# A two-layer decoder trunk in float32 on one core: gathers of the heavy experts five blocks ahead, and two 8 KB tiles as a fifth pair of split weights

## Chip, cores and metric

The kernel runs on one core of one Trainium2 chip. The metric is device time in microseconds (us) of one execution; the median of three executions of the kernel before is 1350.78 us (1350.66 to 1352.81).

## The reference, cut to what matters

256 tokens of width 1024 pass through two residual layers in float32: attention beside a short convolution with a dense SwiGLU, then a gated recurrence with a mixture of experts. The change touches the mixture alone, the last and longest stage:

```python
logits = xf @ w_router                       # 256 tokens, 8 experts
top_logits, top_idx = lax.top_k(logits, 2)
gates = softmax(top_logits)
...
xb = xf[tok]                                 # the tokens of one expert
hb = silu(xb @ w_gate[e]) * (xb @ w_up[e])   # 1024 -> 3584
yb = hb @ w_down[e]                          # 3584 -> 1024
out = zeros.at[row_tok].add(yb * row_gate)
```

Each expert has three matrices of 1024 x 3584 floats. All eight are read whatever the routing: 336 loads of 1 MB.

## The kernel before, in words

**Products in two parts.** A float32 weight tile of 128 x 2048 is split into a high part H, which ScalarE (ACT) writes rounded (L258), and a low part L, the rest, which VectorE (DVE) subtracts (L259). TensorE (PE) multiplies with both. `prepare(n)` (L995) fetches load `n` and splits it.

**Memory of a load.** A load lands in a ring place. There are five tiles of the pool `ring` (`N_RING`, L31) and, by `source` (L978 to 993), two 8 KB tiles of the pool `t8` (`b8`) used in turn with them: seven places in all. Once, in the first round of nine, two loads land in 4 KB halves. A place is free again when DVE has made L from it. The parts H and L go to one of four pairs (`N_HL`, L32; `pair`, L221); a pair is free again when PE has used it.

**Blocks.** The experts are ranked on the chip by their number of tokens. Three heavy ones (0, 3, 6, up to 128 tokens) are worked with 3 matmuls per product, five light ones (1, 2, 4, 5, 7, up to 64) with 2. One block is 512 of the 3584 columns of one expert: 12 pieces (four each of gate `g`, up `u`, down `d`) and 6 loads. The order of the 56 blocks is written out in `experts` (L920 to 928): three heavy blocks, then light, heavy, light again and again. The down pieces of a block come after the gate and up pieces of the next. Expert 1 ends with block 12 and expert 0 with block 13, expert 2 with block 23, experts 3 and 4 with blocks 34 and 33, expert 5 with block 44.

**Other work, by pieces.** The main loop (L1233) multiplies piece `n`, copies out what is pending (`flush`), does what `at` has put down for this piece, and then prepares further loads, up to `(n + 1) // 2 + AHEAD`. All this is one fixed order for each engine. The other work is:

- `choose` (L1011) makes on DVE the matrix of zeros and ones that picks an expert's tokens, and takes the tiles for them;
- `gather` (L1029), four calls, multiplies the tokens with it (L1040 for heavy, L1052 for light experts) into a PSUM tile `pz`, which ACT copies out (L1042, L1057);
- `factors` and `back` (L1062, L1072) prepare the gates and the way back;
- `turn` and `turn_light` (L1111, L1119), five pieces after a block's last `u`, transpose the hidden values through `pz`;
- `out_parts` (L1141) splits an expert's finished sum on ACT and DVE, and `combine` (L1150), four calls from five pieces later on, multiplies it back to the tokens through `pz` (L1155, L1156), and DVE adds it to the residual (L1158).

There are two `pz` tiles. Whoever wants one waits until the one before the last has been read by ACT or DVE.

`experts` places the gathers of a unit of experts that starts at block `s` with `n = s - 3`: `choose` at the last `u` piece of block `n`, the four gathers at pieces `u0`, `u2`, `d0`, `d2` of block `n + 1` (that is `pn(n + 1, "u", 2 * b)`).

The last weights land at about 1326 us; then come the last products, two experts' ends and the output.

Of the kernel before, what the change touches and what calls it, by code (L numbers as in the profile page):

```python
# [9 lines left out]
F32 = mybir.dt.float32  # L10
# [20 lines left out]
N_RING = 5  # L31
N_HL = 4  # L32
# [18 lines left out]

AHEAD = N_HL
FIRST = 1
SECOND = 2
TURN = 5
BACK = 5

TURNS8 = N_RING + 2  # L60
TURNS4 = TURNS8 + 2
ROUNDS = 1

CUT = 4

# [50 lines left out]
def body(ctx, tc, x_d, w_d, prm_d, bv_d, rt_d, out_d):  # L116
# [14 lines left out]
    def nm(s):  # L131
        uid[0] += 1
        return f"{s}_{uid[0]}"

    def b8(dt=F32R):
        return t8.tile([P, 2048], dt, tag="b8", name=nm("b8"))

    def b4(dt=F32):
        return t4.tile([P, 1024], dt, tag="b4", name=nm("b4"))
# [60 lines left out]
    def load(k, w=None, cuts=1):  # L200
        o, n = OFF[k]
        if w is None:
            w = ring.tile([P, 2048], F32, tag="w", name=nm("w"))
        src = w_d[o:o + n * P].rearrange("(p n) -> p n", p=P)
        m = n // cuts
        for c in range(0, n, m):
            nc.sync.dma_start(w[:, c:c + m], src[:, c:c + m])
        return w

    def halves(k):  # L210

        o, n = OFF[k]
        src = w_d[o:o + n * P].rearrange("(p n) -> p n", p=P)
        ws = b4(), b4()
        for i in range(2):
            nc.sync.dma_start(ws[i], src[:, i * 1024:(i + 1) * 1024])
        return ws

    ps = [P0]

    def pair():  # L221
        return [hl.tile([P, 2048], F32R, tag=t, name=nm(t)) for t in "HL"]
# [3 lines left out]
    def split(w, j, n=1024):  # L226

        if j == 0:
            pairs[w.name] = pair()
        c = slice(j * n, (j + 1) * n)  # L230
        h, l = (a[:, c] for a in pairs[w.name])
        with tc.high_priority(offset=ps[0]):
            A.activation(h, w[:, c], AF.Copy)  # L233
            V.tensor_sub(l, w[:, c], h.bitcast(F32))  # L234
        return h, l
# [20 lines left out]
    def hl_of(src, oh, ol):  # L256

        A.activation(oh, src, AF.Copy)  # L258
        V.tensor_sub(ol, src, oh.bitcast(F32))  # L259
# [12 lines left out]
    def norm_factor(spread=True):  # L272

        tot = b2()
        for i in range(4):
            xi = x_sb[:, 2 * i:2 * i + 2, :].rearrange("p k s -> p (k s)")
            if i == 0:
                A.activation(tot, xi, AF.Square)
            else:
                sq = b2()  # L280
                A.activation(sq, xi, AF.Square)
                V.tensor_add(tot, tot, sq)
        p = pz()
        for t in range(2):
            for j in range(2):
                T.matmul(p[:, t:t + 1], tot[:, j * S + t * P:j * S + (t + 1) * P], ones[:, 0:1],
                         start=j == 0, stop=j == 1)
        r = cst.tile([P, 2], F32, name=nm("r"))
        y = rsqrt(p[:, 0:2], 2, 1.0 / D)
        V.tensor_copy(r, y)  # L290
        if not spread:
            return r, None
        dg = b1(F32)
        p = pz()
        for t in range(2):
            V.tensor_scalar(dg[:, t * P:(t + 1) * P], ident, y[:, t:t + 1], None, OP.mult)
            T.matmul(p[:, t * P:(t + 1) * P], ones, dg[:, t * P:(t + 1) * P], start=True, stop=True)
        rs = b1(F32)
        A.activation(rs, p[:, 0:S], AF.Copy)
        return r, rs  # L300
# [85 lines left out]
    for c in range(4):  # L386
        w = wqkv[c]
        for j in range(2):
            k = 2 * c + j
            h, l = split(w, j, 768)  # L390
# [191 lines left out]
    for f in range(NF + 1):  # L582
        cur = None
        if f < NF:
            fb = b8()
            fh, fl = fb[:, 0:1024], fb[:, 1024:2048]
            for i in range(2):
                pg, pu = pw(), pw()
                wide(load(f"fg{f}_{i}"), hT, pg, S)
                if rs is None:  # L590
                    _, rs = norm_factor()
# [321 lines left out]
    def experts(rest):  # L913

        if rest:
            heavy, units = range(NE), [(p,) for p in range(NE)]
# [3 lines left out]
        else:  # L920
            heavy, units = HEAVY, UNITS
            a = [(p, f) for p in HEAVY for f in range(NF)]
            b = [(p, f) for p in LIGHT for f in range(NF)]
            order = a[:LEAD]
            a = a[LEAD:]
            while a or b:
                order += b[:1] + a[:1] + b[1:MIX]
                a, b = a[1:], b[MIX:]
# [13 lines left out]
        def pn(n, m, i):  # L942
            return (12 * n - 4 if n else 0) + {"g": 0, "u": 4, "d": 8}[m] + i

        parts = {}
        loads = len(pieces) // 2
# [16 lines left out]
        def fetch(m, p, f, i, w=None, cuts=1):  # L963
            if rest or p == 0:
                return load(f"m{m}{p}_{f}_{i}", w, cuts)
            if p not in regs:
                regs[p] = nc.values_load(perm[0:1, p:p + 1], engines=[mybir.EngineType.SP], min_val=1, max_val=NE - 1,
                                         skip_runtime_bounds_check_because="a sum over a row with a single one")
            if w is None:
                w = ring.tile([P, 2048], F32, tag="w", name=nm("w"))  # L970
            o = OFF[f"m{m}0_{f}_{i}"][0] - OFF["mg0_0_0"][0]
            src = w_exp[bass.ds(regs[p], 1), o:o + 2048 * P].rearrange("e (p n) -> (e p) n", p=P)
            k = 2048 // cuts
            for c in range(0, 2048, k):
                nc.sync.dma_start(w[:, c:c + k], src[:, c:c + k])
            return w

        def source(n):  # L978

            m, p, f, i = pieces[2 * n]  # L980
            c = n - 2

            if rest:
                return [fetch(m, p, f, i // 2)]
            if c < 0:
                return early[n]
            if c < TURNS4 * ROUNDS:
                c = c % TURNS4
                if c >= TURNS8:
                    return halves(f"m{m}{p}_{f}_{i // 2}")  # L990
            else:
                c = c % TURNS8
            return [fetch(m, p, f, i // 2, b8(F32) if c >= N_RING else None, 2 if loads - n <= CUT else 1)]

        def prepare(n):  # L995

            w = source(n)
            h, l = pair()
            k = 2048 // len(w)
            for i, t in enumerate(w):  # L1000
                cuts = [0, k]
                if loads - n <= CUT:
                    cuts = [0, 1024, 2048] if n < loads - 1 else [0, 1024, 1536, 2048]
                for a, b in zip(cuts, cuts[1:]):
                    c = slice(i * k + a, i * k + b)
                    hl_of(t[:, a:b], h[:, c], l[:, c])
            for i in range(2):
                c = slice(i * 1024, (i + 1) * 1024)
                parts[2 * n + i] = h[:, c], l[:, c]
# [153 lines left out]
        def at(n, fn, *a):  # L1163
            later.setdefault(min(n, len(pieces) - 1), []).append((fn, a))
# [34 lines left out]
        for u, ps in enumerate(units):  # L1199
            s = min(first[p] for p in ps)  # L1200
            if u:
                n = max(s - 3, 0)
                at(pn(n, "u", 3), choose, u)
                for b in range(4):
                    at(pn(n + 1, "u", 2 * b), gather, u, b)
                n = pn(n + 2, "g", 4)
            else:
                n = pn(2, "g", 4)
            for j, p in enumerate(ps):
                at(n + 2 * j, factors, p, slice(0, 2) if u else slice(0, 1))  # L1210
                at(n + 2 * j + 1, back, p)

        with tc.manual_schedule():
            for n in range(FIRST):
                prepare(n)
# [9 lines left out]
            for n in range(FIRST, SECOND):  # L1225
                prepare(n)
# [6 lines left out]
            for n in range(len(pieces)):  # L1233
                products(n)
                flush()
                if n == 1:
                    for b in (1, 3):
                        gather(0, b)
                    flush()
                if n == 0 and not rest:  # L1240
                    norm()
                if n == 3:
                    factors(0, slice(1, 2))
                follow(n)
                for fn, a in later.pop(n, ()):
                    fn(*a)
                while ready < min((n + 1) // 2 + AHEAD, SECOND + n + 1, loads):
                    prepare(ready)
                    ready += 1

    experts(False)

    most = nc.values_load(cnt[0:1, 0:1], min_val=0, max_val=S)
    with tc.If(most > 0):
        experts(True)
# [91 lines left out]
```

## Time and profile before

| what | value |
|---|---|
| median of three executions | 1350.78 us |
| the profiled execution's own time | 1352.24 us |
| its span in the profile | 1350.5 us |
| PE, DVE, ACT busy | 96%, 84%, 72% of the span |
| read from memory | 424.77 MB |
| DMA rate while the experts run | mostly 420 to 423 GB/s, with two dips |

The page gives busy shares by engine and, in 40 slices, the DMA rate. Busy time of PE counts each matmul to a modelled end, and matmuls overlap. A wait stands in the rows as `[time <-who ended it]`. "SPq" is the queue that issues the loads; "us to landing" is the time from the issue of a load to its landing.

### The profile page before, as it was taken

The numbers are of one execution on the slowest core, as the hardware profiler recorded it, in microseconds if no ns is written. First come the engines' busy times: TensorE is split into PE (matmuls) and PEld (weight loads), VectorE is DVE, ScalarE is ACT, GpSimd is POOL, SyncE is SP. The second block draws the span as 40 slices with busy tenths as digits, with TensorE's granted clock in tenths as the row PEclk, the third lists the DMA queues.
The fourth block names the chain that finished last, engine by engine and source line by source line (L and its number), as shares of the span: only waits on it lengthen the run. The fifth ranks groups of instructions, "written<-read, shape, count | busy, mean of one in ns | idle before, by whom it ended". The sixth has DMA issues, their size and how long they took to land.

```text
span 1350.5 us, 19886 instructions
## 1 busy us (share of the span) xinstructions
PE 1301.8 (96%) x7727; PEld 1143.8 (85%) x7727; DVE 1136.4 (84%) x1051; ACT 976.3 (72%) x939; POOL 4.2 (0%) x29
## 2 busy tenths in 40 slices
PE   8899999999998999999989999999998999999997
PEld 7799999999998877888877888878877888878885
DVE  6677655555787788999988999999997999999996
ACT  6445444333587687988877898889886888888884
POOL 1000000000000000000000000000000000000000
PEclk9899999999999899999989999999998999999999
DMA  7444555555433588999998999999998999999993
GB/s 295 148 153 157 187 188 187 180 176 179 180 130 125 203 319 343 401 421 421 421 397 338 408 421 421 413 406 420 421 421 345 363 420 421 422 409 422 421 419 129
DMA packets 61446, 427.19 MB, mean 316 GB/s; under 512 B 7200, under 2 KB 7200, under 8 KB 11296
## 3 DMA queue, kind: packets, MB, share of 16 engines
q1 hardware_dynamic: 60624, 425.22, 79.1%
q8 instruction: 62, 1.02, 0.3%
q10 hardware_dynamic: 720, 0.62, 0.1%
q14 instruction: 40, 0.33, 0.1%
HBM read 424.77 MB, written 1.05 MB: 315 GB/s over the span
## 4 chain that ended last, share of the span: by engine, by line
PE 74%; DVE 12%; ACT 5%; issue 5%; DMA 3%; SPq 0%; ACTq 0%; DVEq 0%
PE pw L239 10%; PE pw L238 10%; PE pw L240 10%; DVE L L259 9%; PE pw L1086 5%; PE pw L1087 5%; PE pz L1125 4%; PE pa L1086 3%; PE pa L1087 3%; PE pa L239 3%; DMA w<-in_w_dram 3%; PE pa L240 3%; PE pa L321 3%; PE pa L238 3%; PE pa L320 3%
## 5 line engine op out<-in xcount | busy, mean ns | idle before, releaser
L259 DVE TENSOR_TENSOR L<-w,H 128x2048 fp32r<-128x2048 f32 (+1 forms) x243 | 537.1, 2242 | 35.3 <-ACT H L258 34.9
L258 ACT ACTIVATE H<-w 128x2048 fp32r<-128x2048 f32 (+1 forms) x243 | 451.1, 1879 | 53.7 <-PE pw L240 19.1
L233 ACT ACTIVATE H<-w 128x1024 fp32r<-128x1024 f32 (+1 forms) x138 | 140.3, 1040 | 153.1 <-issue 139.8
L259 DVE TENSOR_TENSOR L<-b,H 128x2048 fp32r<-128x2048 f32 (+1 forms) x102 | 222.1, 2202 | 8.9 <-ACT H L258 8.8
L1086 PE MATMUL pw<-H,b 128*128 128x512 f32 x560 | 224.1, 400 | 0.0
L1087 PE MATMUL pw<-L,b 128*128 128x512 f32 x560 | 220.9, 394 | 0.2
L234 DVE TENSOR_TENSOR L<-w,H 128x1024 fp32r<-128x1024 f32 (+1 forms) x138 | 164.2, 1205 | 56.0 <-ACT H L233 56.0
L258 ACT ACTIVATE H<-b 128x2048 fp32r<-128x2048 f32 (+1 forms) x102 | 186.8, 1847 | 21.3 <-PE pw L240 9.4
L238 PE MATMUL pw<-b,H 128*128 128x256 f32 x672 | 191.5, 285 | 2.1 <-DVE b L594 1.1
L240 PE MATMUL pw<-b,L 128*128 128x256 f32 x672 | 191.2, 285 | 0.0
L239 PE MATMUL pw<-b,H 128*128 128x256 f32 x672 | 191.1, 285 | 0.0
L238 PE MATMUL pw<-H,b 128*128 128x512 f32 x336 | 134.1, 399 | 0.3 <-ACT b L1173 0.2
L239 PE MATMUL pw<-L,b 128*128 128x512 f32 x336 | 133.0, 396 | 1.3 <-DVE L L259 1.2
L238 PEld LDWEIGHTS pw<-b,H 128*128 128x128 f32 x672 | 129.6, 193 | 3.2 <-issue 2.8
L240 PE MATMUL pw<-H,b 128*128 128x512 f32 x336 | 131.4, 391 | 0.2 <-ACT b L1042 0.2
L239 PEld LDWEIGHTS pw<-b,H 128*128 128x128 f32 x672 | 129.4, 193 | 0.2
L240 PEld LDWEIGHTS pw<-b,L 128*128 128x128 f32 x672 | 129.6, 193 | 0.0
L1087 PEld LDWEIGHTS pw<-L,b 128*128 128x128 f32 x560 | 106.5, 190 | 22.2 <-DVE L L259 1.6
L1086 PEld LDWEIGHTS pw<-H,b 128*128 128x128 f32 x560 | 106.4, 190 | 20.6
L1086 PE MATMUL pa<-H,b 128*128 128x512 f32 x280 | 109.4, 391 | 0.0
L1087 PE MATMUL pa<-L,b 128*128 128x512 f32 x280 | 109.1, 390 | 0.0
L321 PE MATMUL pa<-b,L 128*128 128x256 f32 x352 | 99.5, 286 | 2.7 <-DVE L L234 2.7
(250 smaller groups left out, 1946.1 us busy)
## 6 DMA issues: line engine op xcount, KB each, us to landing
w<-in_w_dram SPq DMA_DIRECT2D x297, 1024.0 KB, 8.9
b<-in_w_dram SPq DMA_DIRECT2D x94, 1024.0 KB, 9.7
w<-in_w_dram SPq DMA_DIRECT2D x12, 512.0 KB, 11.3
b<-in_w_dram SPq DMA_DIRECT2D x8, 512.0 KB, 8.0
w<-in_w_dram SPq DMA_DIRECT2D x4, 768.0 KB, 8.1
x_sb<-in_x_dram SPq DMA_DIRECT2D x4, 256.0 KB, 7.7
out_dram<-x_sb SPq DMA_DIRECT2D x2, 256.0 KB, 2.9
out_dram<-x_sb ACTq DMA_DIRECT2D x2, 256.0 KB, 2.9
```

Of the source, the lines that this page charges most:

```text
L233: A.activation(h, w[:, c], AF.Copy)
L234: V.tensor_sub(l, w[:, c], h.bitcast(F32))
L238: T.matmul(o, a[0], b[0], start=first, stop=False)
L239: T.matmul(o, a[0], b[1], start=False, stop=False)
L240: T.matmul(o, a[1], b[0], start=False, stop=last)
L258: A.activation(oh, src, AF.Copy)
L259: V.tensor_sub(ol, src, oh.bitcast(F32))
L320: T.matmul(o, h[:, c], m[1][:, ks[i], :], start=False, stop=False, skip_group_check=True)
L321: T.matmul(o, l[:, c], m[0][:, ks[i], :], start=False, stop=z and d % 2 == 1, skip_group_check=True)
L1086: T.matmul(o, a, h, start=first, stop=False)
L1087: T.matmul(o, a, l, start=False, stop=last)
L1125: T.matmul(o[:, c:c + 64], src[:, k * P:(k + 1) * P], ii, start=True, stop=True)
```

## The change

Three things change in `experts`.

1. The two 8 KB tiles are no ring places any more: loads land in the five `ring` tiles, except the loads 7 and 8, which land once in halves. Instead, each fifth load (`n % 5 == 4`) is split into the two 8 KB tiles: a fifth pair. `AHEAD` is 5 instead of 4, so load `n` is split one load earlier in the order of ACT and DVE.
2. For units whose first expert is heavy, `n = s - 5` instead of `s - 3`: `choose`, `gather`, `factors` and `back` of experts 3 and 6 come two blocks earlier.
3. All gathers stand one piece later within their block: `u1`, `u3`, `d1`, `d3`.

```diff
-AHEAD = N_HL
+AHEAD = N_HL + 1
...
-TURNS8 = N_RING + 2
-TURNS4 = TURNS8 + 2
-ROUNDS = 1
...
             m, p, f, i = pieces[2 * n]
-            c = n - 2
-
             if rest:
                 return [fetch(m, p, f, i // 2)]
-            if c < 0:
+            if n < 2:
                 return early[n]
-            if c < TURNS4 * ROUNDS:
-                c = c % TURNS4
-                if c >= TURNS8:
-                    return halves(f"m{m}{p}_{f}_{i // 2}")
-            else:
-                c = c % TURNS8
-            return [fetch(m, p, f, i // 2, b8(F32) if c >= N_RING else None, 2 if loads - n <= CUT else 1)]
+            if N_RING <= n - 2 < N_RING + 2:
+                return halves(f"m{m}{p}_{f}_{i // 2}")
+            return [fetch(m, p, f, i // 2, None, 2 if loads - n <= CUT else 1)]
 
         def prepare(n):
 
             w = source(n)
-            h, l = pair()
+
+            h, l = (b8(), b8()) if n % (N_HL + 1) == N_HL else pair()
...
-                n = max(s - 3, 0)
+
+                n = max(s - (5 if ps[0] in heavy and not rest else 3), 0)
                 at(pn(n, "u", 3), choose, u)
                 for b in range(4):
-                    at(pn(n + 1, "u", 2 * b), gather, u, b)
+                    at(pn(n + 1, "u", 2 * b + 1), gather, u, b)
```

What moves on PE, at the end of expert 1 (block 14). Names: `pw` is the sum of a gate or up product, `H` and `L` the split weights, `pz` the small PSUM tile; L1040 is a gather for expert 3, L1155 and L1156 are a combine of expert 1. Before:

```order
L1086 MATMUL pw_6770<-H_6704,b_512_5129 128x512
L1087 MATMUL pw_6770<-L_6705,b_512_5129 128x512
L1040 MATMUL pz_6775<-b_849_6680,b_443_4653 128x128 x8
L1155 MATMUL pz_6784<-b_568_5410,b_855_6698 128x256
L1156 MATMUL pz_6784<-b_568_5410,b_856_6699 128x256
```

Two `pz` tiles are taken one behind the other, by the gather and by the combine, after the same piece.

The same place on PE in the change (lines there stand nine lower from here on: the combine is L1146 and L1147; a fifth pair's parts have names that begin with `b`):

```order
L1078 MATMUL pw_6826<-b_865_6743,b_516_5139 128x512
L1077 MATMUL pw_6826<-b_864_6742,b_516_5139 128x512
L1078 MATMUL pw_6826<-b_865_6743,b_516_5139 128x512
L1146 MATMUL pz_6831<-b_571_5419,b_866_6754 128x256
L1147 MATMUL pz_6831<-b_571_5419,b_867_6755 128x256
```

The combine stands alone; the gather has gone from here.

And where the first gather for expert 3 stands on PE in the change, two blocks earlier (block 12; the gather is L1031):

```order
L1077 MATMUL pw_6542<-H_6456,b_515_5138 128x512
L1078 MATMUL pw_6542<-L_6457,b_515_5138 128x512
L1031 MATMUL pz_6551<-b_803_6450,b_443_4653 128x128 x8
L1077 MATMUL pw_6542<-H_6474,b_515_5138 128x512
L1078 MATMUL pw_6542<-L_6475,b_515_5138 128x512
```

It stands between pieces of a light block, and no combine is near it.

What moves on ACT, at the splits of a few loads near the start (with buffer numbers; `w` is a ring tile, `b8` an 8 KB tile). Before:

```order
L258 ACTIVATE H_594_5522<-b8_593_5520 128x2048
L258 ACTIVATE H_598_5537<-b8_597_5535 128x2048
L1186 ACTIVATE b2_600_5549<-pw_596_5526 128x512
L258 ACTIVATE H_602_5553<-w_601_5551 128x2048
L258 ACTIVATE H_605_5571<-w_604_5569 128x2048
```

Here the 8 KB tiles stand on the right, as places in which a load has landed.

In the change, on ACT, the same stretch:

```order
L254 ACTIVATE H_580_5452<-w_579_5450 128x2048
L254 ACTIVATE b8_583_5470<-w_582_5468 128x2048
L254 ACTIVATE H_586_5488<-w_585_5486 128x2048
L254 ACTIVATE b2_590_5502<-pz_589_5497 128x512
L254 ACTIVATE H_593_5512<-w_592_5510 128x2048
```

They stand on the left, as the high part of every fifth load, and each load has landed in a ring tile.

## Rows read from the trace of the kernel before

**Rows 1.** Windows by stretch: length, PE, PEld, DVE, ACT, POOL busy, clock, DMA share, GB/s.

```profile
560.00:680.00 120.00, 119.13 (x575) 98.85 (x575) 117.86 (x70) 105.12 (x79) 0.00 (x0) 1.00 1.01 421
680.00:760.00 80.00, 73.31 (x369) 61.52 (x368) 70.93 (x49) 61.22 (x51) 0.00 (x0) 0.96 0.94 371
760.00:1000.00 240.00, 237.79 (x1162) 197.13 (x1161) 232.75 (x138) 209.54 (x163) 0.00 (x0) 1.00 1.01 418
1000.00:1080.00 80.00, 73.27 (x364) 61.45 (x363) 70.42 (x50) 60.92 (x49) 0.00 (x0) 0.96 0.94 364
```

**Rows 2.** Timeline of PE, 678 to 690 us: start, length, operation, [idle before <-releaser].

```profile
685.59 1.30 PE L1040 MATMUL pz<-b,b 128*128 128x128 f32 x8 [2.44 <-DVE b L259]
...
688.39 0.58 PE L1155 MATMUL pz<-b,b 128*128 128x256 f32 x1 [1.50 <-DVE x_sb L1158]
```

**Rows 3.** Timeline of the queue SP, single issues of loads: start, length, line.

```profile
653.75 0.34 SPq L975 DMA_DIRECT2D w<-in_w_dram  x1
...
671.19 0.34 SPq L207 DMA_DIRECT2D w<-in_w_dram  x1
...
700.23 0.33 SPq L975 DMA_DIRECT2D w<-in_w_dram  x1
...
719.49 0.33 SPq L975 DMA_DIRECT2D w<-in_w_dram  x1
...
722.29 0.33 SPq L975 DMA_DIRECT2D w<-in_w_dram  x1
...
725.09 0.33 SPq L975 DMA_DIRECT2D w<-in_w_dram  x1
...
863.51 0.33 SPq L975 DMA_DIRECT2D w<-in_w_dram  x1
...
883.18 0.33 SPq L975 DMA_DIRECT2D w<-in_w_dram  x1
...
1021.56 0.33 SPq L975 DMA_DIRECT2D w<-in_w_dram  x1
...
1049.28 0.33 SPq L975 DMA_DIRECT2D w<-in_w_dram  x1
```

**Rows 4.** Issues at 653.75, 700.23, 719.49, 722.29, 863.51, 1021.56: count, size, us to landing.

```profile
w<-in_w_dram SPq DMA_DIRECT2D x1, 1024.0 KB, 13.0
...
w<-in_w_dram SPq DMA_DIRECT2D x1, 1024.0 KB, 6.2
...
w<-in_w_dram SPq DMA_DIRECT2D x1, 1024.0 KB, 5.4
...
w<-in_w_dram SPq DMA_DIRECT2D x1, 1024.0 KB, 5.1
...
w<-in_w_dram SPq DMA_DIRECT2D x1, 1024.0 KB, 7.7
...
w<-in_w_dram SPq DMA_DIRECT2D x1, 1024.0 KB, 8.5
```

**Rows 5.** Timeline of DVE, 640 to 649 us.

```profile
640.39 4.49 DVE L259 TENSOR_TENSOR L<-w,H 128x2048 fp32r<-128x2048 f32 x2
644.79 4.49 DVE L259 TENSOR_TENSOR L<-b,H 128x2048 fp32r<-128x2048 f32 x2
```

**Rows 6.** Groups by line and shape on DVE, 560 to 1320 us: count | busy, mean ns | idle.

```profile
L1158 DVE TENSOR_TENSOR x_sb<-pz,x_sb 128x512 f32<-128x512 f32 x24 | 16.4, 684 | 0.0
L259 DVE TENSOR_TENSOR b<-b,b 128x256 fp32r<-128x256 f32 x33 | 13.8, 418 | 0.0
L1131 DVE TENSOR_TENSOR b<-pz,b 128x256 f32<-128x256 f32 x33 | 13.8, 418 | 0.0
L259 DVE TENSOR_TENSOR b<-pz,b 128x512 fp32r<-128x512 f32 x16 | 10.9, 684 | 0.0
L1182 DVE TENSOR_TENSOR b<-pw,b 128x512 f32<-128x512 f32 x16 | 10.9, 683 | 0.0
L1148 DVE SCALAR_TENSOR_TENSOR b<-pa,gs,b 128x512 fp32r<-128x512 f32 x12 | 8.9, 745 | 0.0
```

## The prediction

> **What bounds the kernel now.** I first cut the experts' stage into stretches [rows 1]. From 560 to 680 and from 760 to 1000 us the transfers run at 421 and 418 GB/s. That is 1.0486 MB in 2.49 us per load, and the DMA share is full (1.01): in these stretches the loads are the bound. In the two stretches between, 680 to 760 and 1000 to 1080, the rate is 371 and 364 GB/s. Against 421 that loses 80 x 50 / 421 = 9.5 us and 80 x 57 / 421 = 10.8 us of transfer time, 20.3 us together. Who stops the queue there?
>
> Next I looked at PE at the start of the first dip [rows 2]. A gather waits 2.44 us for DVE and a combine 1.50 us for DVE: they want a `pz` tile whose last reader stands in DVE's queue behind splits. The clock column shows 0.96 in both dips against 1.00 beside them [rows 1], so about 8% of 80 us, 6.4 us each time, at the lower of the two levels (1.2 instead of 2.4 GHz).
>
> Then I followed single loads [rows 3, 4]. A place is free when the split has ended, and the seventh load after it goes out at that moment. So the time from a landing to the seventh next issue is how long a place is held after the landing; I call it the hold:
> - between dips: issued 653.75, 13.0 to land, landed 666.75, seventh next issue 671.19: hold 4.4 us, just the split itself;
> - first dip: 700.23 + 6.2 = 706.4, next issue 725.09: hold 18.7 us;
> - second dip: 1021.56 + 8.5 = 1030.1, next issue 1049.28: hold 19.2 us;
> - where expert 2 ends: 863.51 + 7.7 = 871.2, next issue 883.18: hold 12.0 us.
>
> How short may issue to landing be with the queue still full? The loads issued at 719.49 and 722.29 took 5.4 and 5.1 us [rows 3, 4] and landed at 724.9 and 727.4, 2.5 us apart. So 5.1 us suffices. With seven places a full queue stands a hold of 7 x 2.49 - 5.1 = 12.3 us. What goes over it is lost for good: 18.7 - 12.3 = 6.4 us in the first dip, 19.2 - 12.3 = 6.9 us in the second, **13.3 us in all**. The other 7 us of the 20.3 I leave as they are.
>
> **The change, part by part.**
>
> *Five places.* A full queue now stands a hold of 5 x 2.49 - 5.1 = **7.3 us** only. The hold between dips is 4.4 us, so the queue stays full there and nothing is lost.
>
> *Gathers elsewhere.* Four gathers of 8 matmuls (1.30 us for one at partly the lower clock [rows 2]; I take 0.9), 3.6 us, leave the pieces where expert 1 is combined, for block 12. Each combine then finds its `pz` tile read two pieces earlier, and I count PE's two waits as gone, and with them the low clock. What stays is DVE's work. From the first `out_parts` of expert 1 (piece 161) to the last combine of expert 0 (piece 184) there are 24 pieces, 12 loads:
> - 12 splits, which follow each other every 2.20 us (644.79 - 640.39 for two [rows 5]): 26.4;
> - the own work of a light and a heavy block [rows 6], less 0.08 of overlap each: 2 x 0.34 + 2 x 0.60 = 1.9;
> - 4 `out_parts` at 0.66 and 8 additions at 0.60 [rows 6]: 7.4.
>
> That is 35.7 us against 12 x 2.49 = 29.9 us of transfers: DVE falls 5.8 us behind, and the hold rises to 4.4 + 5.8 = 10.2 us. Over the limit: **2.9 us** for each dip, 5.8 us for both. Bounds: nothing, if DVE keeps up; 4.4 + 14.3 - 7.3 = 11.4 us each, if the hold rises by 14.3 us as before. I take the sum of DVE's work, since it names all that is left.
>
> *Experts 2 and 5 end.* Half as much: 2 `out_parts`, 4 additions, 3.7 us, and 6 loads with a light block, 13.2 + 0.7 + 3.7 = 17.6 against 14.9: 2.7 behind, hold 7.1, nothing lost. As an upper bound the 12.0 us seen at expert 2 would lose 4.7. I take 1.0 for expert 2, near the sum and not zero since the hold of 12.0 shows more than DVE's sum, and 0.5 for expert 5.
>
> *Start.* Two places fewer, a pair more: one load less can lie ready when the first products begin. That is 2.5 us at most. The fifth pair lets ACT and DVE split a load earlier in the three heavy blocks at the start, where PE is behind; I take 1.2.
>
> *AHEAD 5.* On ACT and DVE the small work of a piece now stands behind one more split. With the loads as the bound, PE runs up to one load (2.5 us) later behind the landings, in the time that the fifth pair gives; the last landing does not move by it. Costs nothing as long as the queue is full; if PE were the bound it would cost up to that 2.5 us once, at the end. Queue SP issues the same loads; the four halves come two loads sooner, before the first product, where the queue waits for places anyhow.
>
> *Gathers of light experts, one piece later.* Their copy on ACT comes behind a split instead of ahead of it. The tokens are needed more than a block later, so nothing waits.
>
> **The sum.** Lost before 13.3; lost after 5.8 + 1.0 + 0.5 + 1.2 = 8.5. Gain 4.8 us. The profiled execution took 1352.24 us (span 1350.5), 1.5 above the median of 1350.78. Taken from the median: **1346.0 us**.
>
> **The rivals.**
>
> *All 13.3 us come back* but for the start: DVE and PE spread their work well enough that no hold passes 7.3 us. For it: the gathers, and the waits behind them, leave. Against: 5.8 us of DVE's work on 2.9 us of room. 1350.8 - 13.3 + 1.2 = 1338.7. Chance 0.15.
>
> *Slower: five places are too few at the ends of the experts.* The first combine after a `turn` still wants the `pz` tile of that `turn`, and its last reader on DVE is now behind one more split. If PE goes on waiting there, and its clock falls again, I take from the rise of 14.3 us only the gathers (3.6) and half their waits (2): 8.7. Then each dip loses 4.4 + 8.7 - 7.3 = 5.8, expert 2 perhaps 2.5, expert 5 1.5, the start 2.5: 18.1 against 13.3, so 1355.6. It decides from a rise of about 8.2 us in a dip on (2 x 5.3 + 2.7 = 13.3). Chance 0.2.
>
> *No change: PE is the bound.* PE is busy 237.79 of 240 us between the dips [rows 1]; if that were its real load, places and pairs would move nothing: 1350.8. Against: PE loses its rate only where a wait is named, and the queue is full at the same time. Chance 0.2.
>
> The Trainium skill (Perfetto Trace Analysis, Identifying the Most-Contended Engine) calls matmul busy time no good measure, because matmuls are pipelined, and takes the busy share of the weight loads. Here that is 197.13 of 240 us, 82%, so by the rule PE has room and the forecast stands at 1346.0; by the busy time itself it would be 1350.8. No run here decides it yet.
>
> That the change does not do what it says I leave out: in the order the gathers for expert 3 stand two blocks earlier, and the 8 KB tiles take splits.
>
> **How the numbers follow.** My case (1342 to 1349) has 0.45, all back 0.15, slower 0.2, no change 0.2. The likeliest is 1346.0. The range takes in the first two and the edge of the slower case: 1338 to 1356. A measurement of this kernel can tell about 0.2%, 2.7 us, from no change. Faster than 1348.1: all of the second and most of the first, 0.57. Within 0.2%: the no-change case and the rest of mine, 0.25. Slower: 0.18.
>
> **What would show it.** Right: in 680 to 760 and 1000 to 1080 PE no longer waits for DVE at a gather or combine, the clock is 1.00, and the rate is some 387 (9.5 - 6.4 + 2.9 = 6.0 us of 80 lost, and 6.8) instead of 371 and 364. The loads take about 8 us to land between dips instead of 13 (five places less a hold of 4.4), at 418 to 421 GB/s as before. Wrong: a rate under 415 between dips (five places do not keep the queue full); a new dip where expert 2 ends, near 865 us; waits of PE on `pz` at the combines of expert 1 as long as now; or a dip before 560 us deeper than one load.

## The result, and the profile after

The change made the kernel slower: a median of 1364.68 us over four executions (1360.31 to 1366.25) against 1351.38 us of before in the same comparison, ratio 1.0092, 95% interval [1.0067, 1.0117]. The forecast was 1346.0 us, in a range of 1338 to 1356: wrong in sign, and out of its range.

The profiled execution took 1360.31 us, the shortest of the four. Its span is 1358.3 us, 7.8 us more than that of before. The windows of the changed kernel answer to [rows 1] (us, busy time and count of PE, PEld, DVE, ACT, POOL, then clock, DMA share, GB/s); the last line is a stretch that [rows 1] have inside 760 to 1000.

```profile
560.00:680.00 120.00, 115.10 (x572) 96.30 (x571) 114.39 (x65) 103.16 (x80) 0.00 (x0) 1.00 1.01 421
680.00:760.00 80.00, 77.85 (x381) 65.28 (x380) 77.43 (x54) 66.19 (x52) 0.00 (x0) 0.98 0.98 382
760.00:1000.00 240.00, 230.26 (x1143) 192.39 (x1142) 229.77 (x136) 207.00 (x162) 0.00 (x0) 1.00 1.01 412
1000.00:1080.00 80.00, 77.87 (x381) 65.17 (x380) 76.80 (x53) 65.65 (x52) 0.00 (x0) 0.98 0.97 382
...
840.00:900.00 60.00, 59.24 (x295) 49.80 (x294) 56.83 (x39) 49.64 (x41) 0.00 (x0) 1.00 1.00 390
```

The same last stretch in the kernel before:

```profile
840.00:900.00 60.00, 59.22 (x292) 49.04 (x291) 58.33 (x38) 51.24 (x40) 0.00 (x0) 1.00 1.01 407
```

The dips are flatter than before (382 and 382 instead of 371 and 364), as forecast, if not by as much. Two things were not forecast: PE is busy 230.26 of 240 us between the dips instead of 237.79, and the rate falls to 390 GB/s where expert 2 ends (407 before).

Where is the time lost? Single loads tell it: issues on the queue SP (start, length, line), and below them, in the same order, the time of each to its landing. First the changed kernel; the last row is the first half of the last load (the last four loads come in halves).

```profile
569.09 0.33 SPq L203 DMA_DIRECT2D w<-in_w_dram  x1
...
695.50 0.33 SPq L971 DMA_DIRECT2D w<-in_w_dram  x1
...
698.30 0.33 SPq L971 DMA_DIRECT2D w<-in_w_dram  x1
...
710.16 0.33 SPq L971 DMA_DIRECT2D w<-in_w_dram  x1
...
850.48 0.33 SPq L971 DMA_DIRECT2D w<-in_w_dram  x1
...
853.88 0.33 SPq L971 DMA_DIRECT2D w<-in_w_dram  x1
...
1323.34 0.33 SPq L971 DMA_DIRECT2D w<-in_w_dram  x1
```

```profile
w<-in_w_dram SPq DMA_DIRECT2D x1, 1024.0 KB, 8.5
...
w<-in_w_dram SPq DMA_DIRECT2D x1, 1024.0 KB, 4.8
...
w<-in_w_dram SPq DMA_DIRECT2D x1, 1024.0 KB, 4.8
...
w<-in_w_dram SPq DMA_DIRECT2D x1, 1024.0 KB, 4.8
...
w<-in_w_dram SPq DMA_DIRECT2D x1, 1024.0 KB, 6.8
...
w<-in_w_dram SPq DMA_DIRECT2D x1, 1024.0 KB, 7.5
...
w<-in_w_dram SPq DMA_DIRECT2D x1, 512.0 KB, 7.2
```

The same two loads in the kernel before, the first (load 42) and the first half of the last: issue, then time to landing.

```profile
563.10 0.33 SPq L207 DMA_DIRECT2D b<-in_w_dram  x1
...
1313.91 0.33 SPq L975 DMA_DIRECT2D w<-in_w_dram  x1
```

```profile
b<-in_w_dram SPq DMA_DIRECT2D x1, 1024.0 KB, 9.2
...
w<-in_w_dram SPq DMA_DIRECT2D x1, 512.0 KB, 11.3
```

- **Start.** Load 42 lands at 569.09 + 8.5 = 577.6 instead of 563.10 + 9.2 = 572.3: 5.3 us late before the first dip begins.
- **Tail.** From the landing of that first half to the end it is 1358.3 - 1330.5 = 27.8 us, before 1350.5 - 1325.2 = 25.3: 2.5 us more.
- **In between**, taken from issue and landing of all 336 loads, as what a stretch takes over 2.485 us a load (1 MB at 422 GB/s): the dips (loads 84 to 114 and 210 to 240) lose 7.8 and 7.6 us instead of 9.5 and 11.1; the ends of expert 2 (144 to 174) and expert 5 (276 to 300) lose 4.8 and 3.0 instead of 1.9 and 0.6.

5.3 - 1.7 - 3.5 + 2.9 + 2.3 + 2.5 = 7.8 us, the whole difference of the spans (the terms are rounded after the subtraction; the stretches left out differ by +0.6 to -0.3 us each and come to nothing together). The other executions, 4 to 6 us longer, are the third run's subject. PE's waits between 560 and 1320 us (us in all, times, longest) show what AHEAD 5 does. The changed kernel, and below it the waits for `pz` of the kernel before:

```profile
PE pa L1077 <- DVE b L255: 23.0, 13, 2.7
PE pz L1146 <- DVE b L255: 3.7, 2, 1.9
PE pz L1031 <- ACT b L1033: 1.1, 2, 0.6
PE pz L1146 <- DVE x_sb L1149: 0.6, 2, 0.3
```

```profile
PE pz L1155 <- DVE x_sb L1158: 5.5, 4, 1.7
...
PE pz L1040 <- DVE b L259: 4.7, 2, 2.4
PE pz L1076 <- DVE gs L1070: 2.6, 3, 1.2
```

The first row is new, and the largest: PE waits up to 2.7 us for the split of a light expert's hidden tile (`split_light`), at 13 of the 33 light tiles of this stretch. On DVE that split now stands behind one load's split more. The waits for `pz` at gathers, factors and combines are down from 12.8 to some 5.5 us. One of 1.9 us at a combine is left in each dip, with the clock at 0.98 there.

### The profile page after: what moved, and what is told of

It reads as the page before. It is cut to its first block, busy times and chain, and to the rows that moved or that the text cites. A ratio compares the mean times of both kernels' runs of the same rounds, so it can differ in the third digit from the quotient of the medians.

```text
span 1358.3 us, 19893 instructions
## 1 busy us (share of the span) xinstructions
PE 1298.1 (96%) x7727; PEld 1144.8 (84%) x7727; DVE 1144.5 (84%) x1051; ACT 980.7 (72%) x939; POOL 4.2 (0%) x29
## 4 chain that ended last, share of the span: by engine, by line
PE 52%; DMA 18%; DVE 12%; ACT 10%; issue 7%; ACTq 0%; SPq 0%; DVEq 0%
DMA w<-in_w_dram 18%; PE pw L234 8%; PE pw L236 8%; PE pw L235 8%; DVE L L255 7%; ACT H L254 5%; PE pa L317 3%; PE pa L316 3%; PE pa L315 3%; PE pw L1077 2%; PE pw L1078 2%; DVE b L255 2%; PE pa L1077 2%; PE pz L1116 2%; PE pa L1078 2%
## 5 line engine op out<-in xcount | busy, mean ns | idle before, releaser
L255 DVE TENSOR_TENSOR L<-w,H 128x2048 fp32r<-128x2048 f32 (+1 forms) x269 | 603.8, 2257 | 34.7 <-ACT H L254 32.8
L254 ACT ACTIVATE H<-w 128x2048 fp32r<-128x2048 f32 (+1 forms) x269 | 507.4, 1891 | 84.4 <-DMA w<-in_w_dram 57.4
L1077 PE MATMUL pw<-H,b 128*128 128x512 f32 x444 | 177.0, 399 | 0.0
L1078 PE MATMUL pw<-L,b 128*128 128x512 f32 x444 | 174.2, 392 | 0.0
L255 DVE TENSOR_TENSOR b<-w,b 128x2048 fp32r<-128x2048 f32 (+1 forms) x68 | 153.4, 2257 | 7.0 <-ACT b L254 6.7
L254 ACT ACTIVATE b<-w 128x2048 fp32r<-128x2048 f32 (+1 forms) x68 | 128.5, 1891 | 20.2 <-DMA w<-in_w_dram 14.9
L234 PE MATMUL pw<-H,b 128*128 128x512 f32 x276 | 110.8, 401 | 2.4 <-DVE b L1173 2.4
L235 PE MATMUL pw<-L,b 128*128 128x512 f32 x276 | 108.4, 393 | 1.2 <-DVE L L255 1.2
L236 PE MATMUL pw<-H,b 128*128 128x512 f32 x276 | 108.4, 393 | 0.2 <-ACT b L1033 0.2
L1077 PE MATMUL pa<-H,b 128*128 128x512 f32 x224 | 89.9, 401 | 16.8 <-DVE b L255 16.8
L316 PE MATMUL pa<-b,H 128*128 128x256 f32 x352 | 99.7, 285 | 1.2 <-DVE b L255 1.2
L315 PE MATMUL pa<-b,H 128*128 128x256 f32 x352 | 99.5, 285 | 1.0 <-ACT b L254 0.6
L1077 PEld LDWEIGHTS pw<-H,b 128*128 128x128 f32 x444 | 84.2, 190 | 16.4
```

What stands on the lines that cost most here:

```text
L234: T.matmul(o, a[0], b[0], start=first, stop=False)
L235: T.matmul(o, a[0], b[1], start=False, stop=False)
L236: T.matmul(o, a[1], b[0], start=False, stop=last)
L315: T.matmul(o, h[:, c], m[0][:, ks[i], :], start=f and d % 2 == 0, stop=False, skip_group_check=True)
L316: T.matmul(o, h[:, c], m[1][:, ks[i], :], start=False, stop=False, skip_group_check=True)
L1077: T.matmul(o, a, h, start=first, stop=False)
```

## The experiments

Each run was compared with the kernel before in the same session (median 1351.4 to 1352.3 us). No run leaves out work.

**1. The gathers alone.** The kernel before, with the change's places for the gathers and its memory as it was:

```diff
-                n = max(s - 3, 0)
+                n = max(s - (5 if ps[0] in heavy and not rest else 3), 0)
...
-                    at(pn(n + 1, "u", 2 * b), gather, u, b)
+                    at(pn(n + 1, "u", 2 * b + 1), gather, u, b)
```

> The kernel before with the second half of the change alone: gathers of heavy experts five blocks ahead and a piece later; seven ring places, four pairs and AHEAD 4 stay. My theory (the hold of a place over what the queue can stand sets the dips): the change's gathers bring the hold in the first dip from 18.7 to about 10 us (9.9 us in the changed kernel), and seven places stand 12.3 us. So both dips (680 to 760 and 1000 to 1080) nearly vanish, 400 GB/s and more in each; the start, the tail and the ends of experts 2 and 5 stay as before. 1350.8 - 6.4 - 6.9 = 1337.5 at best; I expect 1338 to 1343. Rival A (PE is the bound, the gathers only move its work): 1350 to 1352, with dips as before or PE busy as before. Rival B (the gathers' move is itself what harms, for example the split on ACT behind one more step): 1355 to 1365, as the changed kernel.

Measured: 1339.48 us, ratio 0.9909 [0.9893, 0.9924], 12.2 us less than before. The time is what my theory gave. By the landings, the dips lose 4.6 and 5.2 us instead of 9.5 and 11.1, so 10.7 us of the gain arise there. The hold came otherwise than expected (about 10 us). Load 99, issue and time to landing, and the issue that takes its place again:

```profile
708.01 0.34 SPq L975 DMA_DIRECT2D b<-in_w_dram  x1
...
727.71 0.33 SPq L975 DMA_DIRECT2D b<-in_w_dram  x1
```

```profile
b<-in_w_dram SPq DMA_DIRECT2D x1, 1024.0 KB, 5.7
```

It landed at 713.7, so its place was held for 14.0 us; the longest hold of the second dip is 14.7. The windows, columns as above:

```profile
680.00:760.00 80.00, 77.51 (x377) 64.32 (x375) 79.23 (x53) 67.92 (x53) 0.00 (x0) 0.98 1.00 401
760.00:1000.00 240.00, 237.87 (x1181) 198.11 (x1180) 229.50 (x139) 206.54 (x165) 0.00 (x0) 1.00 1.01 418
1000.00:1080.00 80.00, 77.52 (x374) 64.25 (x374) 79.24 (x54) 67.91 (x53) 0.00 (x0) 0.98 0.99 397
```

The dips run at 401 and 397, and DVE is busy 79.2 of 80 us in them: what is left there is DVE's work. PE's busy time between the dips is what it was (237.87 against 237.79), and yet the kernel is 12 us faster, so that busy time is not what sets the kernel's time. That PE has room outside the dips too shows in the changed kernel from 560 to 680: 572 products in 115.10 us busy at 421 GB/s, where the kernel before shows 575 in 119.13 at the same rate. The Trainium skill's rule on the weight loads (Perfetto Trace Analysis, Identifying the Most-Contended Engine) gave PE this room; both runs agree with it.

**2. The memory alone.** The change with these two lines turned back: five places, five pairs, AHEAD 5, gathers as before.

> The change with its gathers put back where they were (three blocks ahead, on even steps): five places, five pairs, AHEAD 5. My theory: it has all that the changed kernel lost (start about 5.3 us, ends of experts 2 and 5 about 5.8, tail 2.5) and the dips' holds of 18.7 and 19.2 against the limit of 7.3 us for five places, so 5 us more in each dip than before: 1350.8 + 5.3 + 5.8 + 2.5 + 2 x 5.0 = 1374, between 1368 and 1380, dips under 360 GB/s. Rival A (with five pairs the gathers do not matter): 1362 to 1367, as the changed kernel. Rival B (the gathers are what cost, the places cost nothing): 1348 to 1353.

Measured: 1378.42 us, ratio 1.0204 [1.0190, 1.0218]. So the two halves of the change pull against each other: memory and order +26.7 us, gathers -12.2 us with seven places and -12.5 with five (against the changed kernel of the same session, the next run). The gathers give the same whatever the places. The windows show what is lost without them, dip by dip:

```profile
680.00:760.00 80.00, 73.63 (x372) 62.17 (x371) 71.77 (x50) 61.93 (x49) 0.00 (x0) 0.96 0.90 350
1000.00:1080.00 80.00, 72.80 (x370) 61.52 (x369) 70.20 (x50) 61.19 (x49) 0.00 (x0) 0.96 0.89 350
```

**3. The changed kernel once more**, unaltered, for a profile of a longer execution.

> The changed kernel once more, unaltered, for a second profile. Its profiled execution took 1360.3 us, the other three 1364 to 1366, with a mean granted clock of 0.988 against 0.980 to 0.983. If the difference is the clock that falls after PE's new waits (PE at the light hidden product waits up to 2.7 us for DVE's split, 13 times between 560 and 1320), a profile at about 1364 shows stretches at 0.9 and less that begin at such a wait, between the dips too. If it is something else (slower transfers), the rate between the dips is under 415 GB/s with the clock at 1.00. Time 1360 to 1367 either way.

Measured: 1365.90 us, ratio 1.0099 [1.0083, 1.0114]; the profiled execution took 1367.49. Its timeline of PE (start, length, operation, [idle before]) at 618 us:

```profile
618.01 0.39 PE L1078 MATMUL pw<-L,b 128*128 128x512 f32 x1
621.22 0.50 PE L1077 MATMUL pa<-H,b 128*128 128x512 f32 x1 [2.82 <-DVE b L255]
621.56 0.40 PE L1078 MATMUL pa<-L,b 128*128 128x512 f32 x1
621.79 0.39 PE L1077 MATMUL pa<-H,b 128*128 128x512 f32 x1
...
622.26 0.63 PE L1077 MATMUL pa<-H,b 128*128 128x512 f32 x1
622.69 0.63 PE L1078 MATMUL pa<-L,b 128*128 128x512 f32 x1
```

and its windows there:

```profile
600.00:620.00 20.00, 18.40 (x89) 14.90 (x87) 19.21 (x11) 17.74 (x15) 0.00 (x0) 1.00 1.02 422
620.00:640.00 20.00, 18.78 (x84) 15.67 (x85) 18.64 (x12) 16.65 (x13) 0.00 (x0) 0.91 1.01 420
640.00:660.00 20.00, 20.00 (x100) 16.84 (x99) 19.80 (x12) 17.18 (x12) 0.00 (x0) 1.00 1.01 409
```

PE waits 2.82 us, and soon after its products stand 0.43 us apart instead of 0.23 and take 0.63 us: it is at the lower of the two levels (1.2 instead of 2.4 GHz) for some 3 us, and the slice shows 0.91. This comes four times outside the dips here (at 622, 810, 906 and 1278 us), each time after a wait at this line of 2.3 to 3.1 us; in the first profile of the change it came once (1318 us), after the same kind of wait. Not every such wait brings it, and not every fall costs time. The span is 7.2 us longer than in the first profile. By the landings, 1.6 us of that are there before load 42 lands, where both profiles show the same falls; nothing is lost around the falls at 622 and 810 us; 2.4 us are lost from load 144 to 174, where the fall at 906 lies, 1.4 from 300 on, after the one at 1278, and 0.9 behind the last landing. So the falls can account for about half of the difference between these two executions; what makes the rest is open.

**4. Five places without the fifth pair.**

```diff
-AHEAD = N_HL + 1
+AHEAD = N_HL
...
-            h, l = (b8(), b8()) if n % (N_HL + 1) == N_HL else pair()
+            h, l = pair()
```

> The change without its fifth pair: five places, four pairs, AHEAD 4, the two 8 KB tiles unused after the start, gathers as in the change. It tells what the places cost from what the pair and AHEAD 5 cost. My theory: the start (5.3 us) and the ends of experts 2 and 5 (5.8 us) are the price of two places less and stay; the tail (2.5 us later after the last landing) and PE's waits for the split of the light hidden product, with the clock that falls behind them (about 4 us), come from AHEAD 5 and go: 1364.7 - 2.5 - 4 = 1358, between 1355 and 1361. Rival (the pair gives back some of what the places cost, so that without it the holds run over 7.3 us more often): 1366 to 1375.

Measured: 1361.37 us, ratio 1.0065 [1.0050, 1.0081], a little over what I expected. Against run 1, which differs in the two places (and in when the four halves come at the start), that is **21.9 us for two ring places**. The tail is back: the first half of the last load was issued at 1327.91 and took 7.1 us, span 1360.7, so 25.7 us. No 20 us slice between 460 and 1320 us has a clock under 1.00.

**5. The fifth pair, but AHEAD 4**: the changed kernel with the first of these two lines only.

> The changed kernel with five pairs but AHEAD 4: the fifth pair is there, the splits stand in the order of before. It parts the pair's memory from the order that AHEAD 5 makes. My theory (the order costs, the memory neither costs nor gives): as the kernel with five places and four pairs, 1359 to 1363; last landing to end 24.5 us instead of 26.5, PE's waits at the light hidden product at most 1.3 us each. Rival A (the pair's memory is worth something by itself, ACT and DVE wait less for PE): 1352 to 1358. Rival B (it is not the order; AHEAD 4 leaves the time as the change has it): 1364 to 1367 and waits of 2.7 us at that product as there.

Measured: 1358.75 us, ratio 1.0051 [1.0036, 1.0066]; the interval overlaps that of run 4, so what the pair's memory gives by itself, nothing or up to 2.6 us, isn't settled. What AHEAD 5 costs is: 1365.3 (the mean of the change's two medians) - 1358.75 = 6.5 us, or 7.3 with each taken against the kernel before of its own session. PE's waits of the row above are all but gone:

```profile
PE pa L1077 <- DVE b L255: 2.8, 7, 0.5
```

**6. Six places**, in the kernel of run 1 (the sixth is taken in turn from the two 8 KB tiles):

```diff
-TURNS8 = N_RING + 2
+TURNS8 = N_RING + 1
```

> Seven places and the change's gathers (1339.5 us), with one place fewer: one of the two 8 KB tiles is taken in turn as the sixth place; four pairs and AHEAD 4 stay. It tests the limit of the hold as a formula: six places stand 6 x 2.49 - 5.1 = 9.8 us. Seven places hold up to 13.3 and 14.6 us in the dips, 12.0 at expert 2's end, 11.4 at expert 5's. My theory: the start loses one load's worth, 2.6; each dip about half of the 3.4 that five places lose more than seven, 1.7; expert 2's end 2.0 and expert 5's 0.8: 1339.5 + 9 = 1348, between 1346 and 1351. Rival A (all or nothing: the sixth place already covers what the holds need): 1339 to 1342. Rival B (the loss is not from places; it comes with the 8 KB tiles being used for something else): 1358 or more, or 1339.

Measured: 1347.20 us, ratio 0.9967 [0.9957, 0.9977]. The price goes by the place: 1339.5, 1347.2 and 1361.4 us with seven, six and five. The rate at expert 2's end and in the second dip:

```profile
840.00:900.00 60.00, 59.24 (x291) 48.73 (x290) 58.49 (x38) 51.46 (x40) 0.00 (x0) 1.00 1.00 399
1000.00:1080.00 80.00, 76.84 (x378) 63.00 (x377) 77.77 (x54) 66.79 (x52) 0.00 (x0) 1.00 0.99 385
```

**7. The light split sooner**, in the changed kernel, to take PE's new waits away:

```diff
-                    at(n + (3 if last else TURN + 3), split_light, p, f)
+                    at(n + (3 if last else TURN + 1), split_light, p, f)
```

> The changed kernel (AHEAD 5, five pairs) with the split of a light expert's hidden tile two pieces sooner (TURN + 1 instead of TURN + 3), so that on DVE it stands ahead of one load's split more. It takes away PE's waits of about 2.7 us at the first product of the light hidden tile, and leaves AHEAD 5. My theory: these waits set off the falls of the granted clock (in the changed kernel's second profile PE waits 2.82 us at 618 to 621 us, and its next products take 0.63 us each instead of 0.39). Without them the 20 us slices between the dips all show a clock of 1.00; the time goes from 1365 to about 1360 (1358 to 1362), the tail of 26.5 us stays. Rival A (the clock falls for another reason, and the waits cost nothing): 1364 to 1367, clock falls between the dips as there. Rival B (the split sooner makes DVE or ACT wait in line for turn_light's product, so that all loads' splits come later): over 1367.

Measured: 1411.04 us, ratio 1.0431 [1.0405, 1.0456]. My theory missed by 50 us, and rival B is what happened. ACT's largest wait (560 to 1320 us) names it:

```profile
ACT b L254 <- DVE b L1122: 81.1, 31, 3.7
```

The split's first half is ACT's, and it needs the product of `turn_light`, which stands on DVE behind a load's split. ACT works in order, so it stands still, and the next loads' splits with it.

**8. Seven places up to load 43, five after**, in the kernel of run 1:

```diff
-            return [fetch(m, p, f, i // 2, b8(F32) if c >= N_RING else None, 2 if loads - n <= CUT else 1)]
+            return [fetch(m, p, f, i // 2, b8(F32) if c >= N_RING and n < 44 else None, 2 if loads - n <= CUT else 1)]
```

> The gathers of the change, four pairs and AHEAD 4, seven ring places up to load 43 (about 575 us), five from there on. It tells the start's share of what the two places cost. My theory: the kernel with five places throughout (1361.4 us) has its loads 5.2 to 5.7 us late from load 42 on, because PE is behind in the heavy blocks at the start and every place less is a load less that lies ready. Here load 42 lands as before (within 1 us), the later losses stay: 1361.4 - 5.3 = 1356, between 1354 and 1358. Rival (what the start gains is given back, for instance because the dips and ends take the lead away): 1360 to 1362. The other way (the places cost only at the start): 1340 to 1345.

Measured: 1356.57 us, ratio 1.0035 [1.0022, 1.0048], 4.8 us less than with five throughout. So the start's share of the price is real and separate. Load 42 lands at 572.6, as before; some 2.5 us of the lead are lost between loads 42 and 84, once the places are fewer.

**9 and 10. The gathers' move in two**: five blocks ahead on the old pieces, and a piece later without going ahead (each is one of the two lines of run 1).

> The kernel before with the gathers of heavy experts five blocks ahead, on the even pieces as before; all else as before. Together with the next run it parts the two halves of the gathers' move, which together gave 1339.5 us. My theory (what counts is that the four gathers for block 12 leave the pieces where expert 1 is combined): most of the 12.2 us come from this half, 1340 to 1343, the dips' hold about 13 us instead of 18.7 and 19.2. Rival (what counts is that a gather and a combine no longer stand in the same piece): 1346 to 1352 here, and most of the gain in the next run.

> The kernel before with the gathers of all experts one piece later (odd pieces), three blocks ahead as before. My theory: the gathers for block 12 still stand among expert 1's combines, PE still has their work there and DVE the same; only the waits for a pz tile get shorter: 1346 to 1350, holds of 15 to 18 us in the dips. Rival (a gather and a combine in one piece were the whole trouble): 1339 to 1342.

Measured: 1341.42 us, ratio 0.9931 [0.9916, 0.9946], and 1348.16 us, 0.9977 [0.9968, 0.9987]. Both as my theory had it: most of the gain comes from taking the gathers of experts 3 and 6 out of the pieces where other experts are combined. The hold peaks at 13.4 and 13.7 us in the first of these runs, at 17.7 and 18.1 in the second.

**11. Turn and split of the light hidden tile sooner**, in the changed kernel:

```diff
-                    at(n + (1 if last else TURN), turn_light, p, f, sg, u)
-                    at(n + (3 if last else TURN + 3), split_light, p, f)
+                    at(n + (1 if last else TURN - 2), turn_light, p, f, sg, u)
+                    at(n + (3 if last else TURN + 1), split_light, p, f)
```

> The changed kernel (AHEAD 5, five pairs) with both steps of a light expert's hidden tile two pieces sooner: the turn (TURN - 2) and the split (TURN + 1). In the run that moved the split alone, ACT waited 81.1 us for DVE's product of the turn (31 times), because that product came behind a load's split; here it comes ahead of that. So PE's waits of about 2.7 us at the first product of the light hidden tile should go without a new wait. My theory: with them go the falls of the granted clock between the dips; 1358 to 1362 instead of 1365, tail 26.5 us as there. Rival A (the falls come without these waits): 1364 to 1367. Rival B (the turn comes too soon: PE, or its weight loads, wait for ACT's copy out of the accumulators at each light block instead): over 1366 and a wait at the turn's transposes.

Measured: 1365.58 us, ratio 1.0113 [1.0097, 1.0130]: no gain. The wait only moved, to where rival B had it, the turn's transposes (PE's largest wait, 560 to 1320 us):

```profile
PE pz L1116 <- ACT b L1177: 10.0, 14, 1.3
```

It is half as long, and the clock falls behind some of these waits just the same; the timeline of PE at 811 us shows one fall:

```profile
812.65 1.18 PE L1116 MATMUL pz<-ii,b 128*128 128x64 f32 x8 [1.21 <-ACT b L1177]
813.59 0.78 PE L1077 MATMUL pa<-b,b 128*128 128x512 f32 x1
814.16 0.63 PE L1078 MATMUL pa<-b,b 128*128 128x512 f32 x1
```

So it is not that line: with AHEAD 5 PE waits at many of the light tiles (14 of 33 here) wherever the hidden tile is made, and falls follow waits as short as these. What the waits cost the run does not tell, since it brought another loss: its first dip loses 13.1 us instead of 7.8, behind a gather's wait of 1.6 us (at 665) and some 7 us at the lower clock. That the falls alone make the 4 to 6 us between executions is not shown; no run took the waits away and left AHEAD 5.

**12. All gathers five blocks ahead**, in the kernel of run 1: `n = max(s - (3 if rest else 5), 0)`.

> The fastest so far (gathers of heavy experts five blocks ahead, a piece later, seven places, four pairs) with the gathers of the light experts five blocks ahead too. The gathers of light experts then stand two blocks sooner. My theory: no hold is over the limit of 12.3 us because of them (12.0 at expert 2's end, 11.4 at expert 5's), so nothing measurable changes: 1337 to 1341. Rival A (they stand in the pieces of the ends of experts 2 and 5, and leave them): 1336 or less. Rival B (they come to stand where an expert is combined now): 1343 or more.

Measured: 1339.58 us, ratio 0.9918 [0.9904, 0.9932]: no difference from run 1, as expected. Run 1 and this one are the fastest of all.

## Why the prediction was wrong, point by point

**Where 18.1 us went.** The forecast was 4.8 us less, the medians show 13.3 more. By the terms of the sum, the dips gave back 2.3 us less than forecast, the ends of experts 2 and 5 cost 3.7 more, the start 4.1 more and the tail 2.5; that makes the 12.6 us by which the first profile misses the forecast. The other 5.5 lie between that profile (7.8 us more than before) and the medians (13.3 more).

**The dips of before: the cause right, the sizes in part by luck.** Holds over what the queue can stand were named as the cause, and taking the gathers away shortened the holds and the dips. But the 13.3 us named as lost and the 12.2 that came back are not the same thing: in run 1 the dips still lose 4.6 and 5.2 us. What came back is the fall of the hold, 18.7 - 14.0 and 19.2 - 14.7, together 9.2 us by the holds and 10.7 by the landings. The hold forecast from DVE's work, 10.2, came in the changed kernel: the load issued at 695.50 landed at 700.3, and its place was issued again at 710.16, a hold of 9.9 us. That is luck too: in run 1, with the same work on DVE and more places, the hold rose to 14.0 and 14.7. Nor did the low clock go: each dip keeps one wait of 1.9 us at a combine, and a clock of 0.98 (0.96 before).

**"So 5.1 us suffices": the step that failed first.** I took two loads that had landed 5.4 and 5.1 us after their issue, 2.5 us apart [rows 3, 4], for proof that the queue stays full at that. Two loads are no rate. In the changed kernel the load issued at 698.30, 4.8 us on its way, landed 2.8 us after the one before it (703.1 - 700.3), and at expert 2's end the load issued at 853.88 landed 4.1 us after the one before it (861.4 - 857.3). Over loads 44 to 329 of the changed kernel, 51 landed within 7 us of their issue, 2.76 us after the load before on average, and 235 later, at 2.53; in the kernel before it was 3.12 (27 loads) and 2.52 (259). I take 7.5, where the kernel before is at 2.50 (250 loads above it). Then seven places stand a hold of 17.4 - 7.5 = 9.9 us, and five stand 4.9, not 7.3: half a microsecond above the split's own 4.4. This also covers most of "the other 7 us", which I left as they were: 18.7 - 9.9 = 8.8 of the 9.5 us in the first dip.

The five profiles with seven places bear the 9.9 out. Their longest holds in the two dips (from issue and landing of all loads), less 9.9, are 8.7 and 9.5 us in the kernel before, 4.1 and 4.8 in run 1, 3.5 and 3.8 in run 9 (five blocks ahead only), 7.8 and 8.2 in run 10 (a piece later only), 3.0 and 3.3 in run 12; the dips lose 9.5 and 11.1, 4.6 and 5.2, 3.7 and 5.3, 9.4 and 8.2, 3.0 and 4.1, in the same order. Less 12.3, run 12's holds would have lost 0.6 and 0.9. With five places the sum falls short (below), and why the queue needs so long is not shown: about half of the 51 loads still came within 2.55 us of the one before, and the mean is raised by single late ones. The time to landing was not varied by itself, but run 6 shows that the loss goes by the place.

- *Dips*, 2.9 us each after the change: they gave back 1.7 and 3.5 us, not 3.5 and 4.0. Peak hold 9.9 less 4.9 is 5.0, and 7.8 and 7.6 us were lost. Five places go round more than twice in the 12 loads of a dip, so the excess may be paid more than once; no run shows that.
- *Experts 2 and 5*, 1.0 and 0.5: measured 2.9 and 2.3. The forecast hold of 7.1 came (7.3); "nothing lost" at it did not follow.

**Start, 1.2: measured 5.3.** Not one load less lies ready, but two, one for each place: 2 x 2.49. As long as PE is behind this doesn't show; once the loads are the bound it is a delay of all that follow. What the fifth pair gives back isn't settled: load 42 lands at 577.4 without it (run 4), at 575.5 with it and AHEAD 4 (run 5), but at 577.6 and 579.2 in the two profiles of the changed kernel, which differ by nearly as much.

**AHEAD 5, "Costs nothing as long as the queue is full": measured 6.5 us.** The 2.5 us at the end that I allowed for PE as the bound came although the loads were it. They come with the order and not with the pair: from the first half of the last load to the end it takes 25.8 us in run 5, which has the pair, and 27.8 and 28.7 in the two profiles of the change. The rest I hadn't seen at all. I had written that small work stands behind one more split, and followed the copies, but not `split_light`, for which PE now waits at 13 of 33 light tiles; behind such waits the clock falls, now and then. That these waits and falls make up the other 4 us is likely, not shown.

**Five places keep the queue full between the dips, as forecast**: 8.0 to 8.5 us to landing, 421 GB/s. The rates forecast for the dips, 387, came as 382. Of the signs that I named for being wrong, three showed: a dip at 865 us, a start deeper than one load, and 412 GB/s in 760 to 1000.

**The rivals.** *All back* comes within a microsecond of run 1 (1338.7 against 1339.5), but by luck: run 1 keeps its places, and its dips still lose 9.8 us. *Slower* had the right cause, too few places, and not the right carrier: it rested on waits for `pz` that stay, and more than half of these went; it left out half of the start, and the tail. *No change* is refuted by run 1.

In sum, by medians: gathers -12.2 us (run 1), two places +21.9 (run 4 less run 1), the fifth pair between -2.6 and 0 (run 5 less run 4), AHEAD 5 +6.5. That gives +13.6 with the pair at -2.6; measured 13.3 and, once more, 14.2. Each of these terms is the step from one run to the next, so they add up by themselves; what they show is the size of each part, in this order of taking them.

## What to carry to other kernels

- Price a buffer in bytes against what each use of it holds up. Here 8 KB as a landing place is worth 8 to 14 us, and 16 KB as a pair of results nothing that can be told. The number of places times the time of one transfer, less the time to landing at which the rate is still full, is the delay that the queue can stand; take that time from many loads, not from the two best. With seven places this gave the loss of ten dips to within 2 us; with five it gave too little.
- Looking further ahead on engines that work in order puts every small product behind one more large one. List all that the critical engine takes from them, not only the copies.
- Parts of a change that have each a sign of their own should be run apart: the gathers alone are 25 us better than the whole.

## What the runs showed of the hardware that was not expected

- Waits of PE of 1.2 to 3.1 us are followed by about 3 us at the lower clock, in some executions and not in others. The times of the changed kernel, with many such waits, spread over 7 us (1360.31 to 1367.49 over eight executions), those of run 1 over 1.4 us; that the clock makes all of this spread is not shown.
- The shortest time from issue to landing of 1 MB in the experts' stage is 4.7 to 4.8 us in the kernel before, the changed one and run 1, about 1.9 transfers' worth, yet the loads that landed within 7 us came 2.7 to 3.1 us apart on average instead of 2.49.
